# Softmax row sums by accumulating DMA transfers instead of GpSimd adds, and every low part of the probabilities on VectorE

## The chip, the core and the metric

One core of a Trainium2 chip runs one launch of the whole kernel. The metric is the device time of that launch in microseconds (us). Engines are named as in the profile: PE is TensorE (PEld its weight loads), DVE is VectorE, ACT is ScalarE, POOL is GpSimd, SP is SyncE.

## What is computed

One layer of a diffusion backbone for 512 latent tokens and 128 context tokens: modulation, a combined input projection, four heads of mLSTM, eight heads of attention, an output projection and an MLP. The change lies in the attention of the latent tokens alone: 512 queries against 512 latent and 128 context keys, all in 32-bit floats.

```python
def one(qi):
    s = jnp.einsum('bqhd,bkhd->bhqk', qi, kf) * scale
    p = jax.nn.softmax(s, axis=-1)
    return jnp.einsum('bhqk,bkhd->bqhd', p, vf)
```

## The kernel before

Weights and activations are cut into a high part (a cast to fp32r) and a low part (the value less its high part), and a product is made of two or three matmuls of these parts. `split` (L108) is the helper: the cast on ACT (L109), the subtraction on an engine that the caller names (L110).

The attention runs over 8 heads h and, in each, over 5 blocks j of 128 keys: a step (h, j). `weights(h, j)` (L978) multiplies the keys of the block by all 512 queries into a PSUM tile `st` (three matmuls, L982 to L984), takes the exponential on ACT into a tile `p` of 128 keys by 512 queries (L986), and splits it into `pu` (hi, lo). The subtraction of block 1 goes to POOL, those of the other four to DVE (L996). The row sum of the softmax needs the sum of the five tiles `p`: POOL adds them one after another into a tile `tot` of a pool of its own (L1001 to L1004, four adds a head). `values(h, j)` (L1007), two steps later, multiplies the values by hi and lo into `pv` (L1013), and with the last block `pvt` (L1017) copies half of it out. `sums(h)` (L1023), two steps after the last block, multiplies `tot` by a column of ones, which adds over the keys (L1027, tile `su`), and DVE takes the reciprocal (L1031). After every second head, `normalise` (L1034) scales the two heads' outputs.

Beside these the same steps prepare the next head: transposes `Tq` and `Tk` (L928, L937), their evacuation on ACT and DVE (L915, L916), a memset on POOL of one row of the key tile (L925), the row maxima `mx`, `nm` (L947, L948), and a context self-attention `cs`, `pc`, `co`. In the last three heads PE also has the first half of two output tiles `wo` (L637) to do, work that needs no attention result.

The tiles `p` and `pvt` come from one ring of 7 buffers (`tp`, tag "t", L89). The order of instructions on each engine is set by the program's scheduler, which uses an estimate of its own for how long things take; once set, every engine works its queue in order, and an instruction that waits holds up all behind it on that engine. A DMA issued on POOL stands in POOL's queue in the same way.

Of the kernel before, what the change touches and what calls it, by code (L numbers as in the profile page):

```python
# [14 lines left out]
ALU = mybir.AluOpType  # L15
# [7 lines left out]
TL = 512  # L23
# [31 lines left out]
def hybrid_layer(ctx: ExitStack, tc: tile.TileContext, d, o):  # L55
    nc = tc.nc
    V, S, G, PE = nc.vector, nc.scalar, nc.gpsimd, nc.tensor
# [20 lines left out]
    def U2(pool, name, dt=F32):  # L78
        return pool.tile([P, 8 * SW], dt, tag="u2", name=name)

    def view(t, off, *shape):
        n = int(np.prod(shape))
        v = t[:, off:off + n]
        if len(shape) == 1:
            return v
        names = "abcd"[:len(shape)]
        return v.rearrange("p (%s) -> p %s" % (" ".join(names), " ".join(names)), **dict(zip(names, shape)))

    def Tt(name, dt=F32, n=T):  # L89
        t = tp.tile([P, 646], dt, tag="t", name=name)  # L90
        return t[:, :n]

    def Pp(name, dt=F32, n=T):
        return tp.tile([P, 646], dt, tag="pp", name=name, bufs=2)[:, :n]
# [7 lines left out]
    def psS(name):  # L102
        return pss.tile([P, 512], F32, tag="s", name=name)

    def f(ap):
        return ap.bitcast(F32)

    def split(hi, lo, src, eng=V):  # L108
        S.copy(hi, src)  # L109
        return eng.tensor_tensor(out=lo, in0=src, in1=f(hi), op=ALU.subtract)  # L110
# [89 lines left out]
    def wget(key, ahead=3):  # L200
        i = state["get"]
        assert chunks[i][0] == key, (chunks[i][0], key)
        wsplit(i + 1)
        wdma(i + 4)
        wsplit(i + ahead)
        state["get"] += 1
        return ready.pop(i)
# [320 lines left out]
    for i in range(NT):  # L528
# [7 lines left out]
                      in_=st[:, KL + ROPE:KL + ROPE + 8].rearrange("p (a b) -> p a b", a=2))  # L536
        V.tensor_copy(out=gf[:, i, :].rearrange("p (a b) -> p a b", a=2)[:, :, 0:4],
                      in_=st[:, KL + ROPE + 8:KL + ROPE + 16].rearrange("p (a b) -> p a b", a=2))
# [48 lines left out]
    for ci, row in enumerate((r_a, r_e, r_w)):  # L587
        nt = NT if ci < 2 else 4
        pc = psS(f"pcol{ci}")
        for i in range(nt):  # L590
            PE.transpose(out=pc[:, i * 64:(i + 1) * 64], in_=row[:, i * P:(i + 1) * P], identity=ident[0:64, 0:64])
        V.tensor_copy(out=cols[:, ci, 0:nt].rearrange("p t d h -> p (t d) h"),
                      in_=pc[:, 0:nt * 64].rearrange("p (t b) -> p t b", b=32)[:, :, 0:4])
# [8 lines left out]
    for w in range(2):  # L602
# [4 lines left out]
                        in1=gs.unsqueeze(1).broadcast_to([P, NT, 2, 16]), op=ALU.mult)  # L607
# [195 lines left out]
    for k in range(2):  # L803
        pt = psD(f"ckt{k}")
        for i in range(NT):
# [17 lines left out]
                    in0=krn[:, 0:4].rearrange("p t (a b) -> p t a b", a=2)[:, :, ::-1, :],  # L823
                    in1=sg_[:, 1, 0:4].rearrange("p t (a b) -> p t a b", a=2), op=ALU.mult)
# [9 lines left out]
    for hf in range(2):  # L834
# [4 lines left out]
        hi, lo = wget(("kup", hf))  # L839
# [19 lines left out]
        for i in range(6):  # L859
            G.tensor_tensor(out=kn[:, i, :, 0:NOPE], in0=kn[:, i, :, 0:NOPE], in1=rsk[:, i, :].unsqueeze(2).broadcast_to([P, 4, NOPE]), op=ALU.mult)  # L860
            G.tensor_tensor(out=kn[:, i, :, NOPE:QK], in0=krr[:, i:i + 1, :].broadcast_to([P, 4, ROPE]),
                            in1=rsk[:, i, :].unsqueeze(2).broadcast_to([P, 4, ROPE]), op=ALU.mult)
# [12 lines left out]
    for hf in range(2):  # L875
# [4 lines left out]
        for i in range(NT):  # L880
            ps = (psS if i % 2 else psD)(f"qu{hf}{i}")
            for k in range(3):
                hi, lo = w0 if k < 2 else w1
# [8 lines left out]
            if i < 4:  # L892
                rt = view(Pp(f"rt{hf}{i}"), 0, 4, ROPE)
                V.tensor_tensor(out=rt.rearrange("p h (a b) -> p h a b", a=2),
                                in0=p4[:, :, NOPE:QK].rearrange("p h (a b) -> p h a b", a=2)[:, :, ::-1, :],
                                in1=sg_[:, 0, i:i + 1, :].rearrange("p t (a b) -> p t a b", a=2).broadcast_to([P, 4, 2, 16]), op=ALU.mult)
# [15 lines left out]
    prep, negm, cden, punit, tot, pacc = {}, {}, {}, {}, {}, {}  # L912
# [65 lines left out]
    def weights(h, j):  # L978
        qh, ql_, kh, kl_, qc, kc = prep[h]
        ps = psS(f"st{h}{j}")  # L980
        c = slice(j * P, (j + 1) * P)
        PE.matmul(ps, lhsT=kh[0:QK + 1, c], rhs=qh[0:QK + 1], start=True, stop=False)  # L982
        PE.matmul(ps, lhsT=kh[0:QK, c], rhs=ql_[0:QK], start=False, stop=False)
        PE.matmul(ps, lhsT=kl_[0:QK, c], rhs=qh[0:QK], start=False, stop=True)  # L984
        pj = Tt(f"p{h}{j}", n=TL)
        exp_ = S.activation(out=pj, in_=ps, func=AF.Exp)  # L986
        if h % 2:
            if j in (0, 2):
                u2s[j // 2] = view(U2(php, f"pu{h}{j}", F32R), 0, 5, TL)
            hi, lo = (u2s[j // 2][:, 2 * (j % 2) + k] for k in range(2)) if j < 4 else (u2s[k][:, 4] for k in range(2))  # L990
        else:
            pool, tag = ((whp, "wh"), (wlp, "wl"))[(5 * (h // 2) + j) % 2]
            u = pool.tile([P, 1024], F32R, tag=tag, name=f"pu{h}{j}")
            hi, lo = u[:, 0:TL], u[:, TL:2 * TL]
        punit[h, j] = hi, lo
        lo_ = split(hi, lo, pj, G if j == 1 else V)  # L996
        if j == 0:
            tot[h] = pj
        else:
            if j == 1:  # L1000
                first, tot[h] = tot[h], Pp(f"tot{h}", n=TL)  # L1001
            else:
                first = tot[h]
            G.tensor_tensor(out=tot[h], in0=first, in1=pj, op=ALU.add)  # L1004
        return exp_, lo_

    def values(h, j):  # L1007
# [53 lines left out]
    for n in range(len(steps) + DN):  # L1061
        if n < len(steps):
            h, j = steps[n]
            if h == 7 and j == 0:
                wsplit(state["get"] + 3)
            if (h, j) == (7, 4):
                w_first = wget(("out", 0))
                ps_first = psD("wo0")
                mmT(ps_first, w_first, kview(mhu * 2), kview(mlu * 2), KT, 0, 4)
            exp_, lo_ = weights(h, j)  # L1070
            if (h, j) in MSP:

# [27 lines left out]
        if 0 <= n - DN < len(steps):  # L1100
            h, j = steps[n - DN]
# [313 lines left out]
```

## Time and profile before

| | us |
|---|---|
| median of 3 runs (lowest, highest) | 888.99 (888.43, 892.16) |
| the profiled execution's own time | 886.29 |
| its span, first to last instruction | 884.2 |
| PE busy | 855.6 (97%) |
| DVE busy | 615.1 (70%) |
| ACT busy | 436.5 (49%) |
| POOL busy | 298.0 (34%) |

The profiled execution is 2.7 us below the median of the runs, and 2.1 us of its time lie outside its span. Busy shares are averages over stages with different limits; the steps of the change all lie in the attention, from about 300 to 396 us of the span.

### The profile page before, as it was taken

What the parts mean: (1) busy time and instruction counts of PE and PEld (TensorE: products, weight loads), DVE (VectorE), ACT (ScalarE), POOL (GpSimd) and SP (SyncE); (2) the same over time, 40 slices, a digit from 0 to 9 for tenths busy, and PEclk for the clock granted to TensorE, in tenths of its full rate; (3) what the DMA queues carried; (4) which work ended last, traced back from release to release, by engine and by line L of the source; (5) the groups of instructions that cost most, each with busy time, mean ns of one, the idle gap of its engine ahead of it and who ended that gap; (6) DMA issues with size and microseconds to landing.
All of it is one profiled execution on the core that took longest, in us unless ns stands there. A gap on an engine that the chain in (4) does not pass through costs nothing.

```text
span 884.2 us, 15211 instructions
## 1 busy us (share of the span) xinstructions
PE 855.6 (97%) x5805; PEld 800.7 (91%) x5805; DVE 615.1 (70%) x1226; ACT 436.5 (49%) x959; POOL 298.0 (34%) x311
## 2 busy tenths in 40 slices
PE   6999999999889999999989999999999999999998
PEld 5688799999777677889989999999999999999998
DVE  2654634546787889977898587595876949678673
ACT  3424326535764597955557153361544517254440
POOL 3100113313333575753743152241514215152300
PEclk9999999999999999999999999999999999999999
DMA  9842842231216200322141212122122221412132
GB/s 357 321 131 67 293 166 91 64 99 52 96 57 239 96 1 1 120 72 72 49 144 46 98 49 96 48 96 96 49 96 81 88 72 56 135 49 73 48 102 90
DMA packets 22328, 89.63 MB, mean 101 GB/s; under 512 B 3144, under 2 KB 3944, under 8 KB 18928
## 3 DMA queue, kind: packets, MB, share of 16 engines
q1 hardware_dynamic: 19440, 81.95, 26.8%
q0 software_dynamic: 1664, 4.26, 1.6%
q10 hardware_dynamic: 1152, 2.46, 0.7%
q8 instruction: 46, 0.75, 0.4%
q14 instruction: 26, 0.21, 0.1%
HBM read 85.33 MB, written 3.32 MB: 100 GB/s over the span
## 4 chain that ended last, share of the span: by engine, by line
PE 80%; DVE 8%; DMA 6%; ACT 3%; issue 2%; SPq 1%; POOL 0%; DVEq 0%; POOLq 0%; ACTq 0%
PE dn L637 25%; PE qk L637 6%; PE wo L637 5%; DMA st<-in_w_ada 3%; PE mo L637 2%; PE pv L1013 2%; DMA ad<-in_w_ada 2%; PE ada L389 2%; PE n L702 1%; PE up12M L1235 1%; PE up8M L1235 1%; PE up14M L1235 1%; PE up15M L1235 1%; PE up7M L1235 1%; PE up13M L1235 1%
## 5 line engine op out<-in xcount | busy, mean ns | idle before, releaser
L109 ACT CAST wh<-st 128x1024 fp32r<-128x1024 f32 (+4 forms) x69 | 69.3, 1007 | 103.0 <-PE dn L637 33.1
L1118 DVE SCALAR_TENSOR_TENSOR xr<-dn,modT,xr 128x320 f32<-128x320 f32 x64 | 35.3, 551 | 107.1 <-PE dn L637 107.1
L110 DVE TENSOR_TENSOR wl<-st,wh 128x1024 fp32r<-128x1024 f32 (+4 forms) x67 | 83.3, 1246 | 28.8 <-ACT wh L109 27.8
L637 PE MATMUL dn<-fh,wh 128*128 128x320 f32 x448 | 102.7, 310 | 0.3 <-ACT fh L1278 0.3
L637 PE MATMUL dn<-fh,wl 128*128 128x320 f32 x448 | 102.0, 309 | 0.0
L637 PE MATMUL dn<-fl,wh 128*128 128x320 f32 x448 | 98.6, 309 | 0.0
L109 ACT CAST wu<-S 128x512 fp32r<-128x512 f32 x64 | 38.1, 616 | 99.0 <-issue 92.3
L637 PEld LDWEIGHTS dn<-fh,wh 128*128 128x128 f32 x448 | 74.8, 188 | 2.2 <-PE dn L637 1.6
L637 PEld LDWEIGHTS dn<-fh,wl 128*128 128x128 f32 x448 | 74.9, 188 | 0.0
L637 PEld LDWEIGHTS dn<-fl,wh 128*128 128x128 f32 x448 | 74.0, 188 | 0.0
L1273 POOL TENSOR_TENSOR r<-r,rbs 128x320 f32<-128x320 f32 x32 | 37.5, 1183 | 106.6 <-DVE r L1251 106.6
L110 DVE TENSOR_TENSOR wu<-S,wu 128x512 fp32r<-128x512 f32 x64 | 57.5, 908 | 1.1 <-ACT wu L109 0.9
L1277 ACT ACTIVATE r<-r 128x192 f32<-128x192 f32 (+2 forms) x96 | 40.8, 466 | 25.8 <-DVE r L1251 17.1
L729 POOL TENSOR_TENSOR W<-ngb,mask 128x128 f32<-128x128 f32 x40 | 19.5, 502 | 67.0 <-DVE p L739 33.3
L1280 DVE TENSOR_TENSOR fl<-r,fh 128x320 fp32r<-128x320 f32 x56 | 38.2, 700 | 3.0 <-ACT r L1279 3.0
L1004 POOL TENSOR_TENSOR tot<-tot,p 128x512 f32<-128x512 f32 x24 | 37.2, 1549 | 5.9 <-ACT p L986 3.9
L109 ACT CAST wu<-pair 128x512 fp32r<-128x512 f32 x24 | 14.1, 615 | 43.8 <-PE dn L637 41.6
L110 DVE TENSOR_TENSOR pu<-p,pu 128x512 fp32r<-128x512 f32 x32 | 33.0, 1045 | 2.5 <-ACT pu L109 2.5
L219 POOL TENSOR_TENSOR S<-st,st 128x512 f32<-128x512 f32 x8 | 13.0, 1627 | 59.8 <-DVE wu L110 59.8
L1013 PE MATMUL pv<-pu,v 128*128 128x512 f32 x80 | 29.1, 427 | 2.1 <-DVE pu L110 2.0
L637 PE MATMUL wo<-mh,wh 128*128 128x320 f32 x128 | 29.6, 311 | 0.7 <-DVE xr L1120 0.7
L637 PE MATMUL qk<-hh,wl 128*128 128x320 f32 x128 | 29.9, 312 | 0.0
(487 smaller groups left out, 2436.8 us busy)
## 6 DMA issues: line engine op xcount, KB each, us to landing
st<-in_w_ada SPq DMA_DIRECT2D x16, 1024.0 KB, 5.6
st<-in_w_down SPq DMA_DIRECT2D x32, 512.0 KB, 3.4
ad<-in_w_ada SPq DMA_DIRECT2D x8, 1024.0 KB, 17.5
st<-in_w_up SPq DMA_DIRECT2D x16, 512.0 KB, 3.8
pair<-in_w_up SPq DMA_DIRECT2D x16, 512.0 KB, 4.8
st<-in_w_qko SPq DMA_DIRECT2D x12, 512.0 KB, 3.6
st<-in_w_out SPq DMA_DIRECT2D x8, 512.0 KB, 3.3
x<-in_x SPq DMA_DIRECT2D x4, 640.0 KB, 6.7
```

Of the source, the lines that this page charges most:

```text
L109: S.copy(hi, src)
L110: return eng.tensor_tensor(out=lo, in0=src, in1=f(hi), op=ALU.subtract)
L389: PE.matmul(ps[32 * j:32 * j + 32, 0:n], lhsT=sz[:, 2 * q + k, :], rhs=w[:, k, c], start=q == 0, stop=q == 3, tile_position=(0, 32 * j))
L637: PE.matmul(out[:, hf * 512:hf * 512 + HT], lhsT=wt[:, c], rhs=xt[k][:, hf * HT:(hf + 1) * HT], start=k0 == 0 and n == 0, stop=k1 == nk an ...
L729: G.tensor_tensor(out=W[:, dg:dg + P], in0=nb_[dr][:, j * P:(j + 1) * P], in1=mask[:, dr, :], op=ALU.add)
L1004: G.tensor_tensor(out=tot[h], in0=first, in1=pj, op=ALU.add)
L1013: PE.matmul(pacc[h], lhsT=v_u[hf][:, j, hh_, :], rhs=w, start=j == 0 and k == 0, stop=j == 4 and k == 1)
L1118: V.scalar_tensor_tensor(out=xr[m][:, 0:HT], in0=ps[:, 0:HT], scalar=modT[:, gi_ + m, 0:1], in1=xr[m][:, 0:HT], op0=ALU.mult, op1=ALU.add)
L1235: PE.matmul(ps, lhsT=w[:, c], rhs=b[k], start=k == 0 and w is hi and b is bh, stop=k == 3 and w is lo)
L1273: E.tensor_tensor(out=t, in0=t, in1=rbs[:, c], op=ALU.mult)
L1277: S.activation(out=t[:, c0:c1], in_=t[:, c0:c1], func=AF.Relu, bias=r[n][:, w:w + 1])
L1280: V.tensor_tensor(out=FL[n][:, c], in0=t, in1=f(FH[n][:, c]), op=ALU.subtract)
```

## The change

The adds on POOL are gone. The tile `p` of block 0 becomes the accumulator itself, and each of the other four blocks is added to it by a DMA, issued on POOL, that reads `p` of the block and adds it onto the destination. The low part of block 1 is made on DVE, as the others are. The separate tile `tot` falls away.

```diff
@@ -993,15 +993,12 @@
             u = pool.tile([P, 1024], F32R, tag=tag, name=f"pu{h}{j}")
             hi, lo = u[:, 0:TL], u[:, TL:2 * TL]
         punit[h, j] = hi, lo
-        lo_ = split(hi, lo, pj, G if j == 1 else V)
+        lo_ = split(hi, lo, pj)
         if j == 0:
             tot[h] = pj
         else:
-            if j == 1:
-                first, tot[h] = tot[h], Pp(f"tot{h}", n=TL)
-            else:
-                first = tot[h]
-            G.tensor_tensor(out=tot[h], in0=first, in1=pj, op=ALU.add)
+
+            G.dma_start(out=tot[h], in_=pj, accum_op=ALU.add)
         return exp_, lo_
```

From L1004 on, lines of the changed kernel have numbers lower by 3 (the add of L1004 is the DMA of L1001, `su` of L1027 is L1024).

POOL's queue from head 0 to the start of head 1, before. Names carry head and block (`p01` is head 0, block 1); in brackets stand the engines or DMA transfers (DMASW) waited for.

```order
L1004 TENSOR_TENSOR tot0_3291<-p00_3265,p01_3286 128x512 [waits DMASW6_49,Activation_49]
L110 TENSOR_TENSOR pu01_3288<-p01_3286,pu01_3288 128x512 [waits Activation_49]
L1004 TENSOR_TENSOR tot0_3291<-tot0_3291,p02_3314 128x512 [waits Activation_49,Pool_49]
L925 MEMSET qk2_3384 1x640 [waits PE_49,Pool_49]
L1004 TENSOR_TENSOR tot0_3291<-tot0_3291,p03_3336 128x512 [waits Activation_49,Pool_49]
L1004 TENSOR_TENSOR tot0_3291<-tot0_3291,p04_3361 128x512 [waits Activation_49,Pool_49]
L1004 TENSOR_TENSOR tot1_3406<-p10_3379,p11_3402 128x512 [waits DMASW7_49,Activation_49]
```

The same place in the changed kernel.

```order
L1001 DMA p00_3265<-p01_3286 128x512 [waits DMASW2_49,DVE_49]
L925 MEMSET qk2_3383 1x640 [waits PE_49,Pool_49]
L1001 DMA p00_3265<-p02_3313 128x512 [waits DMASW3_49,DMASW2_49,Activation_49]
L1001 DMA p00_3265<-p03_3335 128x512 [waits DMASW3_49,Activation_49]
L1001 DMA p00_3265<-p04_3360 128x512 [waits DMASW4_49,Activation_49]
L1001 DMA p10_3378<-p11_3401 128x512 [waits DMASW6_49,DVE_49]
L1001 DMA p10_3378<-p12_3440 128x512 [waits DMASW7_49,DMASW6_49,Activation_49]
```

The adds are DMAs now; the second, third and fourth of a head each wait for the transfer of the one before them, while the first waits for DVE (the low part of block 0, which reads the accumulator before it is changed) and not for the last transfer of the head before.

PE's queue around the row sum of head 0, before.

```order
L982 MATMUL st11_3398<-qk1_3270 128x512
...
L961 MATMUL cs1_3418<-qkc1_3271 128x128 [waits PE_49]
L947 MATMUL mx20_3449<-qk2_3384 128x320 [waits Activation_49]
...
L1027 MATMUL su0_3430<-ones_99,tot0_3291 128x2 [waits Activation_49,Pool_49]
...
L982 MATMUL st12_3438<-qk1_3270 128x512 [waits Activation_49]
...
L947 MATMUL mx21_3453<-qk2_3384 128x320 [waits DVE_49]
```

The same place in the changed kernel.

```order
L982 MATMUL st11_3397<-qk1_3270 128x512
...
L961 MATMUL cs1_3416<-qkc1_3271 128x128 [waits PE_49]
L947 MATMUL mx20_3447<-qk2_3383 128x320 [waits Activation_49]
...
L947 MATMUL mx23_3471<-qk2_3383 128x320 [waits DVE_49]
...
L1024 MATMUL su0_3428<-ones_99,p00_3265 128x2 [waits DMASW5_49]
...
L982 MATMUL st12_3436<-qk1_3270 128x512
...
L1010 MATMUL pv1_3455<-pu10_3380,v0_2616 128x512 [waits Activation_49]
```

The row sum of head h still stands between blocks 1 and 2 of head h + 1, with three more row maxima ahead of it, and waits for the transfer of block 4 in place of POOL; the scores of blocks 2, 3 and 4 of the next head stand behind it. The place is the same in every head but the last.

## Rows read from the trace of the kernel before

**Rows 1.** The page: busy tenths, granted clock and DMA share in 40 slices.

```profile
PE   6999999999889999999989999999999999999998
...
PEclk9999999999999999999999999999999999999999
DMA  9842842231216200322141212122122221412132
```

**Rows 2.** Busy time of each engine between the row sums of heads 0, 1, 4, 7.

```profile
core 0: us, PE busy (x) PEld busy (x) DVE busy (x) ACT busy (x) POOL busy (x), PEclk, DMA share, GB/s
312.35:322.85 10.50, 10.50 (x65) 8.61 (x63) 8.75 (x15) 9.52 (x22) 8.14 (x6) 1.00 0.00 1
322.85:359.00 36.15, 33.82 (x206) 26.52 (x204) 34.13 (x46) 30.14 (x64) 24.35 (x19) 1.00 0.00 1
359.00:394.35 35.35, 35.35 (x230) 29.40 (x229) 32.52 (x44) 27.96 (x57) 23.97 (x17) 1.00 0.34 120
```

**Rows 3.** The chain that ended last, in order of time: row sums.

```profile
312.35 0.79 PE su L1027 x8
...
322.85 0.79 PE su L1027 x8
...
359.00 0.79 PE su L1027 x8
...
394.35 0.79 PE su L1027 x8
```

**Rows 4.** Groups of instructions between 300 and 396 us (count, busy us, mean ns, idle before).

```profile
L1004 POOL TENSOR_TENSOR tot<-tot,p 128x512 f32<-128x512 f32 x24 | 37.2, 1549 | 5.9 <-ACT p L986 3.9 <-ACT mix L976 1.0
L110 DVE TENSOR_TENSOR pu<-p,pu 128x512 fp32r<-128x512 f32 x32 | 33.0, 1045 | 2.5 <-ACT pu L109 2.5
...
L1004 POOL TENSOR_TENSOR tot<-p,p 128x512 f32<-128x512 f32 x8 | 12.2, 1519 | 16.5 <-ACT p L986 13.5 <-DVE mix L1048 3.0
L110 POOL TENSOR_TENSOR pu<-p,pu 128x512 fp32r<-128x512 f32 x8 | 11.1, 1384 | 5.8 <-ACT pu L109 5.8
```

**Rows 5.** Instructions on tile p: shortest, median and longest, ns.

```profile
L986 ACT ACTIVATE p<-st x40: 582/597/617, 301.4 to 392.0; 128x512 f32<-128x512 f32 x40
...
L110 DVE TENSOR_TENSOR pu<-p,pu x32: 671/1038/1784, 303.9 to 393.3; 128x512 fp32r<-128x512 f32 x32
```

**Rows 6.** Timeline of head 0's first low part, and around head 1's row sum.

```profile
303.94 0.68 DVE L110 TENSOR_TENSOR pu<-p,pu 128x512 fp32r<-128x512 f32 x1
...
322.69 0.95 PE L1027 MATMUL su<-ones,tot 128*128 128x2 f32 x8
...
323.78 1.20 DVE L110 TENSOR_TENSOR pu<-p,pu 128x512 fp32r<-128x512 f32 x1
323.88 0.40 PE L982 MATMUL st<-qk 97*128 97x512 f32 x1
...
324.35 0.39 PE L984 MATMUL st<-qk 96*128 96x512 f32 x1
```

**Rows 7.** DMAs issued on POOL: KB each, median us from issue to landing.

```profile
ngb<-ngd POOLq DMA_DIRECT2D x8, 320.0 KB, 3.8
...
cst<-in_C POOLq DMA_DIRECT2D x4, 128.0 KB, 2.6
out_C<-co POOLq DMA_DIRECT2D x4, 128.0 KB, 2.2
...
late<-in_late POOLq DMA_DIRECT2D x1, 256.0 KB, 4.1
```

**Rows 8.** L671, eight 320 KB loads on POOL: issue time (ns), and us to landing.

```profile
L671 POOL DMA_DIRECT2D ngb<-ngd x8: 551/568/608, 104.2 to 222.5; - x8
...
DMA to landing us min/median/max: 3.5/3.8/7.5
```

**Rows 9.** L584, and POOL's timeline there: a DMA waiting for another's landing.

```profile
DMA to landing us min/median/max: 4.5/4.5/4.5
...
99.33 0.51 POOL L584 DMA_DIRECT2D ngd<-ru  x1
99.82 0.50 POOL L585 DMA_DIRECT2D ngd<-ru  x1
104.15 1.11 POOL L671 DMA_DIRECT2D ngb<-ngd  x2 [3.83 <-DMA ngd<-ru]
```

## The prediction

> **What bounds the kernel now.** I read the 40 slices first: PE is busy for nine tenths or more in most of them, its granted clock is full in all, and the DMA engines stand nearly still in slices 15 and 16, which lie in the first half of the attention [rows 1]. All that the change touches lies there, so I went on to the attention alone. The chain of waits shows the row sums of heads 0 and 7 at 312.35 and 394.35 us [rows 3]: 82.0 us for seven heads, 11.7 us a head. Busy time by stretch says what fills them: of the 82.0 us PE works 79.7, and is idle for 2.3 only, all of it in the middle stretch, where DVE works 34.1 of 36.2 us [rows 2]. So the stage is PE's, with DVE close behind, and POOL (56.5 of 82.0 us) has slack. This fixes the most that relief of any other engine can bring here: about 2.3 us.
>
> **What is taken away.** POOL loses 32 adds (37.2 + 12.2 us) and 8 subtractions (11.1 us) [rows 4]. POOL is not the limit, so this is worth nothing by itself. It may help DVE: its subtraction takes 0.67 us at best and 1.05 us in the mean [rows 4, 5]. If POOL's work causes all of that spread, 32 subtractions win 32 x 0.37 = 12 us of DVE time; if none of it, nothing. The 8 subtractions that DVE takes over cost 8 x 0.67 = 5.4 to 8 x 1.05 = 8.4 us. DVE's balance thus lies between -6.6 and +8.4 us, over a stage in which PE, on the sum below, waits far longer for something else. I count it at nothing; without that cover, up to 8 us of it would show, since DVE is idle for only 2 us of the middle stretch.
>
> **What is added: a chain of transfers.** Before, four adds of 1.5 us stood one behind another [rows 4]. Now each is a transfer whose successor waits, at the head of POOL's queue, until it has landed; the first transfer of the next head is not held. At the far end PE's row sum waits for the fourth, and behind that row sum in PE's queue stand the scores of blocks 2, 3 and 4 of the next head, without which the next head's second transfer has nothing to add. Head after head closes a loop: landing, row sum, scores, exponential, three transfers, landing.
>
> Call L the time from the issue of one transfer to its landing. A link is L plus the time until the waiting DMA starts. The trace has one such pair: issued at 99.33 us, landed 4.5 us later, at 103.83, and the waiting DMA starts at 104.15 [rows 9]. A link is L + 0.3.
>
> *First head.* Its first transfer waits for the low part of block 0, done at 303.94 + 0.68 = 304.6 us [rows 6]. Four transfers with three gaps: the fourth lands at 305.5 + 4L.
>
> *Each further head.* From landing to the next head's second transfer: the row sum 0.95 us, the scores 0.86 (323.88 to 324.74) [rows 6], the exponential 0.60 [rows 5], and some 0.4 for the handovers (0.24 lies between row sum and scores [rows 6]): 2.8 us. The first transfer of that head was issued behind the fourth of the last and has landed by then. Three transfers and two gaps follow: 3L + 0.6. A head takes 3L + 3.4.
>
> *Sum.* The row sum of head 7 comes at 305.5 + 4L + 7 x (3L + 3.4) = 329.3 + 25L, against 394.35: a shift of 25L - 65. What follows that row sum is the same work as before, so the shift goes through to the end. PE's own 11.7 us a head fit into the loop's wait as soon as 3L + 3.4 exceeds 11.7, that is from **L = 2.8 us** on.
>
> *How large is L?* No accumulating transfer is in this trace. The plain ones of POOL's queue bound it: 2.2 to 2.6 us for 128 KB, 3.5 to 3.8 for 320 KB, 4.1 for the one of 256 KB, 7.5 for the slowest [rows 7, 8]. From 2.4 at 128 KB to 3.65 at 320 KB is 1.25 us for 192 KB; a plain 256 KB would take 3.2. Here the destination has to be read as well, another 256 KB, 1.7 us at that slope. I take **L = 4.9**, an estimate from these rows, since a plain transfer of the same size already took 4.1. Ends: 2.2, if the second read is free and SBUF at both ends is quick, and 7.5 or more, if the additions run slower than the copies.
>
> With L = 4.9 the shift is 57.5 us: 886.3 + 57.5 = 943.8 for the profiled execution, which stands 2.7 us below the median shown. **I predict 946 us.** A head would take 18.1 us.
>
> The Trainium skill, DMA: Bandwidth & Descriptors, section "Anatomy of one DMA — SWDGE (gpsimd) path", gives 2.0 us plus bytes over 436 GB/s, an estimate of 2.6 us for 256 KB. By it the loop would be shorter than PE's work and the change free, the first rival below. The trace does not agree with it: for 320 KB it would be 2.75, measured were 3.5 at best [rows 8].
>
> *What else moves.* The issue of a transfer holds POOL for about 0.57 us (8 loads of 128 rows, 551 to 608 ns [rows 8]); it runs inside L. The memset for the head after next stands between two transfers and waits out one link; ACT's evacuation of the transposes waits for it, but that is needed only by the next head's scores, most of a loop later. The ring of 7 buffers now holds each tile until its transfer has landed, and the accumulator until the row sum; blocks 2 to 4 of the next head come after that row sum, so they find the older transfers landed. If they did not, one more link a head, about 5 us, would join the loop. In heads 5 to 7 PE's first half of the output tiles now stands before the row sum of head 6 and fills a wait; it brings nothing, as the loop, not PE, sets the end.
>
> **The rivals.** *No change: the transfers are quick* (L of 2.2 to 2.6, from the 128 KB rows [rows 7]). Then PE keeps 11.7 us a head, and only the first chain shows: at 2.6 it lands at 315.9 instead of 312.35, at 2.2 at 314.3. The time is 891 to 893. It decides below L = 2.8. For it: the DMA engines are idle in the first half of the stage [rows 1]. Against it: twice the size of those rows, and a second read. Beyond it lies a gain, of at most PE's 2.3 idle us [rows 2], if DVE's relief is real and the first chain is covered.
>
> *The second read is hidden*: L = 3.2, a plain 256 KB. Shift 15, time 904, still slower.
>
> *The additions are slow*: L above 7.5. At 7.5 the shift is 122 and the time 1011; each further microsecond costs 25. For it: one 320 KB load took 7.5 [rows 8]. Against it: that one left together with a second [rows 9], and in the first half of this stage other traffic is 1 GB/s [rows 2]. DVE might also hold up POOL's making of descriptors: it is busy for 34.1 of 36.2 us [rows 2], yet the issues in the trace spread by 57 ns only [rows 8].
>
> The Trainium skill, SBUF — State Buffer, section "SBUF: two separate sides", says that a DMA issued from GpSimd can sit without descriptors while VectorE runs an operation that holds the port the two share. No run here shows such a case yet; it would make L longer, and so speaks against the change.
>
> **How the numbers follow.** The forecast, L between 2.8 and 7.5, gets 0.80; of this 0.15 is the hidden second read. Additions slower than that get 0.10, quick transfers 0.10: 0.07 for no change and 0.03 for a gain. The range runs from 898 (L of about 3, from 25 x 3 - 65 = 10) to 1015 (7.6) and leaves out the two end cases. A measurement of this kernel tells about 0.5%, 4.4 us, from no change. Faster 0.03, same 0.07, slower 0.90.
>
> **What the profile after would show.** Right: POOL's adds and its `pu` rows gone; `su` rows about 18 us apart; PE idle before `su`, released by a DMA, for some 6 us a head; 32 transfers on POOL of 256 KB with a median landing near 4.9 us; POOL's second, third and fourth DMA of a head waiting for a DMA; the stretch after the last `su` as long as before. DVE's `pu` subtractions nearer 0.67 us would show the relief. Wrong would be: `su` 11.7 us apart and PE still full (quick transfers); or PE waiting for ACT or DVE before the scores, with the transfers long landed (the ring or DVE took over); or a head of 3L + 3.4 that does not fit the landing time measured, which would break the loop itself.

## The result and the profile after

The changed kernel takes **937.1 us** (median of four runs, 931.4 to 938.2), the kernel before 888.7 (887.8 to 892.2): a ratio of 1.0546 [1.0514, 1.0578]. The profiled execution took 937.72 us, with a span of 935.9 against 884.2 before, 51.7 us more.

The page of the changed kernel: the span, TensorE's 40 slices and its granted clock, then two of its groups and one kind of transfer.

```profile
span 935.9 us, 15214 instructions
...
PE   6999999999899779777998999999999999999998
...
PEclk9999999999999798778998999999999999999999
...
L110 DVE TENSOR_TENSOR pu<-p,pu 128x512 fp32r<-128x512 f32 x40 | 27.0, 682 | 14.4 <-ACT pu L109 14.2
L1024 PE MATMUL su<-ones,p 128*128 128x2 f32 x64 | 12.3, 315 | 25.0 <-DMA p<-p 24.7
...
p<-p POOLq DMA_DIRECT2D x32, 256.0 KB, 3.3
```

Four things stand against the rows of before. PE waited 24.7 us for transfers before the row sums. Its slices show holes at 7 where they were full, and there the *granted clock* has fallen too [rows 1]. VectorE's 40 subtractions take 27.0 us, less than the 33.0 of 32 before [rows 4]. And a transfer lands in 3.3 us, not in the 4.9 of the sum.

The stretches of the changed kernel from each row sum to the next (heads 0 to 7), then three stretches behind the last one.

```profile
core 0: us, PE busy (x) PEld busy (x) DVE busy (x) ACT busy (x) POOL busy (x), PEclk, DMA share, GB/s
319.25:334.55 15.30, 14.06 (x58) 11.03 (x58) 4.69 (x8) 8.28 (x17) 3.20 (x4) 0.73 0.36 64
334.55:351.10 16.55, 11.09 (x64) 8.81 (x64) 12.39 (x22) 10.94 (x24) 4.62 (x6) 0.90 0.40 69
351.10:366.35 15.25, 15.14 (x77) 11.84 (x78) 5.81 (x10) 7.80 (x15) 3.20 (x4) 0.77 0.36 63
366.35:383.91 17.56, 11.91 (x66) 8.95 (x66) 14.53 (x24) 13.49 (x30) 4.62 (x6) 0.95 0.38 66
383.91:407.61 23.70, 17.13 (x80) 12.40 (x80) 11.66 (x19) 10.59 (x22) 3.77 (x5) 0.72 0.60 161
407.61:427.47 19.86, 19.86 (x115) 17.21 (x116) 11.10 (x16) 11.18 (x20) 3.43 (x4) 0.87 0.49 109
427.47:440.94 13.47, 6.98 (x32) 4.54 (x30) 2.95 (x5) 4.45 (x9) 2.99 (x8) 0.84 0.45 98
440.94:456.00 15.06, 14.32 (x87) 13.39 (x88) 4.83 (x11) 3.87 (x5) 0.00 (x0) 0.80 0.00 1
...
504.00:508.00 4.00, 3.40 (x15) 2.58 (x13) 4.00 (x8) 1.89 (x5) 1.59 (x2) 0.62 0.02 6
508.00:512.00 4.00, 3.96 (x17) 3.96 (x17) 1.98 (x5) 1.01 (x2) 0.00 (x0) 0.53 0.00 0
```

The seven stretches make 121.7 us where before had 82.0 [rows 3]. With the first row sum 6.9 us late, the last one is 46.6 us late (440.94 against 394.35). From there to the end it takes 495.0 us against 489.9, 5.1 more, and 46.6 + 5.1 = 51.7 is the whole difference. Of the 5.1 us, 2.8 are lost by the first matmul of the MLP (496.8 against 447.4); the row 440.94:456.00 shows TensorE busy there at a clock of 0.80. The rest is lost behind it, where from 504 to 512 us the clock is low once more (0.62 and 0.53), after TensorE had been idle for 1.8 us for ScalarE and not for a transfer.

POOL's timeline of the changed kernel (start, duration, the idle time before with its releaser): the loop from head 0 to head 1, the first transfer of head 2, a disturbed transfer of head 5, and the second transfers of heads 6 and 7.

```profile
315.89 1.75 POOL L1001 DMA_DIRECT2D p<-p  x2 [2.96 <-DMA p<-p]
323.53 0.86 POOL L1001 DMA_DIRECT2D p<-p  x1 [5.88 <-ACT p L986]
327.33 0.86 POOL L1001 DMA_DIRECT2D p<-p  x1 [2.94 <-DMA p<-p]
331.14 0.86 POOL L1001 DMA_DIRECT2D p<-p  x1 [1.89 <-ACT pu L109]
336.33 0.86 POOL L1001 DMA_DIRECT2D p<-p  x1 [4.33 <-DVE rd L1028]
...
397.98 0.86 POOL L1001 DMA_DIRECT2D p<-p  x1 [2.63 <-ACT qk L955]
411.89 0.86 POOL L1001 DMA_DIRECT2D p<-p  x1 [8.60 <-ACT p L986]
...
430.15 0.86 POOL L1001 DMA_DIRECT2D p<-p  x1 [6.07 <-ACT p L986]
```

This is the loop that was forecast. The pair at 315.89 is head 0's fourth transfer and head 1's first. The fourth lands at 319.2, the row sum runs at 319.25, the scores and the exponential follow, and head 1's second transfer leaves at 323.53, then one every 3.8 us. Head 1's row sum is at 334.55. A link is 3.3 + 0.5 us, not L + 0.3. The transfer at 397.98 landed after 9.6 us, beside two loads of 1,280 KB that SP issued at 396.58.

### The profile page after: what moved, and what is told of

It is laid out like the page before. It is cut to its first block, busy times and chain, and to the rows that moved or that the text cites. A ratio compares the mean times of both kernels' runs of the same rounds, so it can differ in the third digit from the quotient of the medians.

```text
span 935.9 us, 15214 instructions
## 1 busy us (share of the span) xinstructions
PE 879.7 (94%) x5805; PEld 817.1 (87%) x5805; DVE 607.8 (65%) x1234; ACT 437.8 (47%) x959; POOL 265.1 (28%) x303
## 4 chain that ended last, share of the span: by engine, by line
PE 50%; DVE 2%; issue 1%; DMA 0%; ACT 0%; DVEq 0%; POOLq 0%
PE dn L637 24%; PE wo L637 4%; PE up1M L1232 1%; PE up12M L1232 1%; PE up4M L1232 1%; PE up8M L1232 1%; PE up14M L1232 1%; PE up15M L1232 1%; PE up7M L1232 1%; PE up13M L1232 1%; PE up11M L1232 1%; PE up9M L1232 1%; PE up5M L1232 1%; PE up3M L1232 1%; PE up10M L1232 1%; PE up2M L1232 1%
## 5 line engine op out<-in xcount | busy, mean ns | idle before, releaser
L1001 POOL DMA_DIRECT2D p<-p x32 | 27.6, 893 | 105.8 <-ACT p L986 46.6
L986 ACT ACTIVATE p<-st 128x512 f32<-128x512 f32 x40 | 23.8, 598 | 47.6 <-PE st L984 46.6
L110 DVE TENSOR_TENSOR pu<-p,pu 128x512 fp32r<-128x512 f32 x40 | 27.0, 682 | 14.4 <-ACT pu L109 14.2
L1024 PE MATMUL su<-ones,p 128*128 128x2 f32 x64 | 12.3, 315 | 25.0 <-DMA p<-p 24.7
L1024 PEld LDWEIGHTS su<-ones,p 128*128 128x128 f32 x64 | 11.9, 276 | 26.9 <-DMA p<-p 26.2
L1010 PE MATMUL pv<-pu,v 128*128 128x512 f32 x80 | 32.2, 467 | 1.5 <-ACT pu L109 1.1
## 6 DMA issues: line engine op xcount, KB each, us to landing
ad<-in_w_ada SPq DMA_DIRECT2D x8, 1024.0 KB, 17.5
```

Of the source, the lines that this page charges most:

```text
L1001: G.dma_start(out=tot[h], in_=pj, accum_op=ALU.add)
L1010: PE.matmul(pacc[h], lhsT=v_u[hf][:, j, hh_, :], rhs=w, start=j == 0 and k == 0, stop=j == 4 and k == 1)
L1024: PE.matmul(ps[:, 2 * i:2 * i + 2], lhsT=t[:, i * P:(i + 1) * P], rhs=ones[:, 0:2], start=True, stop=True)
```

## Experiments

**e1_low_only** does one half of the change alone: VectorE makes all low parts, the additions stay on POOL.

```diff
-        lo_ = split(hi, lo, pj, G if j == 1 else V)
+        lo_ = split(hi, lo, pj)
```

> The kernel before, with only the low part of block 1 moved from GpSimd to VectorE; the adds stay on GpSimd. Theory (the chain of transfers is the whole loss): no measurable change, 886 to 892 us against 889, and VectorE's 40 subtractions take 0.8 to 1.05 us each. Rival (the eight more subtractions on VectorE, which was busy 34.1 of 36.2 us in the middle stretch, cost their time): 894 to 897 us.

Measured: 893.9 us against 887.5, 1.0067 [1.0044, 1.0091], 6.4 us more: nearly what the rival said. The waits of e1_low_only from 300 to 420 us (total, times, longest).

```profile
PEld pv L1013 <- DVE pu L110: 9.0, 15, 1.4
...
PE pv L1013 <- DVE pu L110: 4.0, 9, 0.9
```

VectorE's eight further subtractions are not hidden where POOL still adds: the mean of all 40 is 1,039 ns there, against 682 in the changed kernel. In e2_dma_only below, where POOL keeps its subtractions and has no additions, it is 688 ns. So it is POOL's *additions* that stretch VectorE's subtractions, not POOL's subtractions.

**e2_dma_only** does the other half: transfers as in the change, block 1's low part back on POOL.

```diff
-        lo_ = split(hi, lo, pj)
+        lo_ = split(hi, lo, pj, G if j == 1 else V)
```

> The changed kernel with the low part of block 1 back on GpSimd; the sums stay with the accumulating transfers. Theory: the whole loss is here, 932 to 945 us, a little above the changed kernel if GpSimd's 1.3 us subtraction lands between two links. Rival (the low part shares in the loss): 925 us or less.

Measured: 940.7 us, 1.0593 [1.0557, 1.0629], about as long as the whole change (the intervals overlap). The loss lies in the transfers.

**e4_plain_copy** takes the addition out of the transfers: they overwrite their destination.

```diff
-            G.dma_start(out=tot[h], in_=pj, accum_op=ALU.add)
+            G.dma_start(out=tot[h], in_=pj)
...
```

The row sums are therefore left out, and VectorE clamps what it finds at 1.0, one small instruction more a head (not shown in the cut; e10_half has it too).

> The changed kernel with plain copies in place of the accumulating transfers: each overwrites the accumulator, so the row sums are left out (VectorE clamps what it finds, off the path); same sizes, queue and waits. Theory (reading the destination is priced as I forecast, with a good part of the transfer): the copies land in 2.4 us or less against 3.3, and the time falls by 20 us or more. Rival (the addition itself costs next to nothing, fixed parts make up the 3.3): 3.0 to 3.3 us to landing, an issue near 0.57 us instead of 0.86, and 928 to 938 us.

Measured, in one run: 907.9 us against 888.1. The transfers of e4_plain_copy (ns of an issue, then us to landing):

```profile
L1001 POOL DMA_DIRECT2D p<-p x32: 536/538/632, 303.2 to 411.7; - x32
...
DMA to landing us min/median/max: 2.2/2.3/7.4
```

The addition costs 3.3 - 2.3 = 1.0 us of each landing, of which 0.32 in the issue (857 ns against 538 at the median). But a loss of 20 us is left at 2.3 us, where the prediction's sum had none.

**e10_half** sends only half the columns (128 KB).

```diff
-            G.dma_start(out=tot[h], in_=pj, accum_op=ALU.add)
+            G.dma_start(out=tot[h][:, 0:TL // 2], in_=pj[:, 0:TL // 2], accum_op=ALU.add)
...
```

> The changed kernel with each accumulating transfer cut to half of the columns (128 KB); the second half of the row sums is that of block 0 alone, VectorE clamps the sums at 1.0. The plain copies of 256 KB landed in 2.3 us, the accumulating ones in 3.3. Theory (the addition costs by the byte, and the price is the loop's): landing falls by half of that 1.0 us, to 2.7 to 2.9 us; each of some 25 links is 0.4 to 0.6 shorter, 10 to 15 us, and the clock gives some back: 918 to 928 us. Rival (the addition is a fixed cost of each transfer, as is most of the landing): 3.1 to 3.3 us and 932 to 939 us.

Measured: 916.9 us, 1.0334 [1.0304, 1.0364], and this landing in the trace of e10_half:

```profile
DMA to landing us min/median/max: 2.6/2.7/6.5
```

Half the bytes save 0.6 us of 3.3, so the larger part of a landing is not paid by the byte. The landing is what the theory said, the time a little lower. That the addition costs by the byte is not shown: its 0.32 us in the issue stay (857 ns at the median here too), and a plain copy of 128 KB, which would split the 0.6 us into copy and addition, was not run. The three runs are a sweep over L: 2.3 gives +19.8 us, 2.7 gives +29.0, 3.3 gives +48.4 (by the medians). That is 23 and 32 us per microsecond of landing. The prediction's 25 lies between them; its zero, at L = 2.6, was wrong.

**e7_fill** asks what the clock does. Before each set of row sums PE runs 14 matmuls of 512 columns into the same bank, which the row sums overwrite; they need no transfer and run while PE would wait.

```diff
+        for i in range(14):
+            PE.matmul(ps, lhsT=identr, rhs=v_u[0 if h < 3 else 1][:, 0].rearrange("p a b -> p (a b)"), start=True, stop=True)
         for i in range(4):
             PE.matmul(ps[:, 2 * i:2 * i + 2], ...
```

> The changed kernel with 14 idle-filling matmuls of 512 columns ahead of each row sum on TensorE, into the PSUM bank that the row sum then overwrites (3.3 us of work a head that computes nothing). Theory (part of the loss is TensorE's clock, 0.50 for several microseconds after each long wait): the granted clock stays at 1.0 or nearly, the row sums and scores take 0.95 and 0.86 us again, and the time falls by 5 to 12 us in spite of the added work. Rival (the clock only slows work that has slack): 937 us or more.

Measured: 920.6 us, 1.0364 [1.0327, 1.0401]: **16.5 us less** than the changed kernel (the theory said 5 to 12), with 27.7 us more work on its bottleneck engine. But the filling is not all that differs. With it the scheduler chose another order; TensorE's timeline of e7_fill around the first row sum:

```profile
313.47 3.42 PE L1024 MATMUL su<-v,kc 128*128 128x512 f32 x14
316.73 0.39 PE L982 MATMUL st<-qk 97*128 97x512 f32 x1
...
318.47 0.40 PE L982 MATMUL st<-qk 97*128 97x512 f32 x1
...
321.18 1.05 PE L1026 MATMUL su<-ones,p 128*128 128x2 f32 x8 [1.38 <-DMA p<-p]
```

The scores of blocks 2 and 3 of head 1 stand ahead of head 0's row sum here, and not behind it. The same holds for one block at head 2's row sum and for two at head 5's; at the others the scores stay behind. So e7_fill also opens the loop in three of seven heads, and its gain is not the clock's alone. The stretches of e7_fill between its row sums (four of the seven; columns as above):

```profile
321.18:334.72 13.54, 12.48 (x62) 9.71 (x62) 6.88 (x12) 7.33 (x16) 3.77 (x5) 0.87 0.46 79
...
350.71:364.28 13.57, 13.57 (x92) 11.38 (x90) 8.77 (x14) 10.02 (x21) 3.74 (x5) 1.00 0.39 69
364.28:378.54 14.26, 14.09 (x78) 11.35 (x77) 11.27 (x18) 11.73 (x24) 4.06 (x5) 1.00 0.43 75
...
418.07:432.42 14.35, 14.35 (x78) 11.60 (x77) 3.24 (x6) 4.67 (x9) 2.80 (x5) 1.00 0.32 56
```

Where the clock is full, a head takes 13.6 to 14.4 us. The prediction's 3L + 3.4 gives 13.3 for the L of 3.3 that was measured; of these stretches the last two keep the forecast order of row sum and scores. The last row sum is at 432.42, 8.5 us earlier than in the changed kernel, and from there to the end it takes 489.6 us, about as before the change; but 20 more of the output projection's matmuls, some 3 us, stand ahead of that row sum here, 68 in place of 48.

How the clock falls without the filling, in the changed kernel around the first row sum (columns as above):

```profile
312.00:313.00 1.00, 0.35 (x2) 0.30 (x2) 1.00 (x2) 0.95 (x3) 0.85 (x1) 1.00 0.00 0
313.00:314.00 1.00, 0.81 (x4) 0.30 (x2) 1.00 (x3) 1.00 (x4) 0.00 (x0) 0.89 0.57 100
...
316.00:319.00 3.00, 0.00 (x0) 0.00 (x0) 0.64 (x1) 0.00 (x0) 1.64 (x2) 0.50 0.58 99
...
323.00:327.00 4.00, 4.00 (x15) 3.12 (x14) 1.39 (x2) 2.07 (x4) 0.86 (x1) 0.50 0.36 66
327.00:328.00 1.00, 1.00 (x8) 0.95 (x7) 0.00 (x0) 0.27 (x1) 0.67 (x1) 0.79 0.00 0
```

The clock is down to 0.50 (1.2 of 2.4 GHz) when PE stands still for the transfer, and stays there while PE is busy without a pause from 320 to 327 us. The wait is thus paid a second time: the row sum takes 1.87 us where it took 0.95, and what stands behind it runs slower too, inside the loop. The changed kernel itself has the price. From the row sum to the second transfer of the next head it takes 4.28 us in heads 1, 3, 5 and 6, at 0.50 (319.25 to 323.53), and 2.68 in head 7 (427.47 to 430.15), where the clock was full:

```profile
319.25:323.53 4.28, 4.28 (x14) 3.80 (x15) 0.18 (x1) 0.86 (x2) 0.00 (x1) 0.50 0.24 42
427.47:430.15 2.68, 2.68 (x18) 2.36 (x17) 0.18 (x1) 0.86 (x2) 0.00 (x0) 1.00 0.58 197
```

That is 4 x 1.6 = 6.4 us inside the loop, for the same row sum, scores and exponential.

**e6_xr_late** asks what the loads beside the transfers cost. The two loads of 1,280 KB are held back until the last normalisation.

```diff
     for k in range(2):
+        V.tensor_copy(out=view(xu2[k], 0, 4, T)[:, 0, 0:1], in_=mix_a[:, 3, 0:1])
         nc.sync.dma_start(out=view(xu2[k], 0, 4, T), ...
```

> The changed kernel with the two 1280 KB loads of the residual held back until the last head is normalised (a one-column copy into each buffer makes them wait). Theory (they lengthened two links, to 9.6 and 6.2 us, and the chain is the path): all links of heads 5 and 6 that lay beside them are near 3.3 us again and the time falls by 6 to 10 us, to 927 to 931, less what the later loads cost the output projection. Rival (those links were hidden): 935 us or more.

Measured: 934.8 us, 1.0522 [1.0489, 1.0555], hardly less than the changed kernel and nearly what the rival said. The chain that ended last in e6_xr_late, transfers of heads 5, 6 and 7 and, later, the load:

```profile
396.25 3.25 DMA p<-p
...
409.37 6.17 DMA p<-p
...
416.61 6.11 DMA p<-p
...
443.51 5.58 DMA xr<-in_x
```

Without the loads head 5's landings are back at 3.3 us (396.25, where 9.6 stood). Two later ones still take 6.1 to 6.2, beside the loads of the output projection's weights, which I did not move. The last row sum comes 6.8 us earlier (434.11), and 5.7 us of it are given back behind it, where the chain now waits for the late load. So the lengthened landings are real, but moving these loads buys nothing.

**e5_two_acc** shortens the chain: blocks 1 and 2 are added to block 0, block 4 to block 3, 24 transfers, and PE's row sums add the two accumulators.

```diff
-        if j == 0:
-            tot[h] = pj
+        if j in (0, 3):
+            tot[h, j > 2] = pj
...
+            for k in range(2):
+                PE.matmul(ps[:, 2 * i:2 * i + 2], lhsT=t[k][:, i * P:(i + 1) * P], rhs=ones[:, 0:2], start=k == 0, stop=k == 1)
```

> The changed kernel with two accumulators a head: blocks 1 and 2 are added to block 0, block 4 to block 3, and the row sum adds both on TensorE; 24 transfers, the longest chain two. Theory (the loop is as long as its chain): the fourth link and the third fall away, landing and block 4's exponential are 4 to 5 us apart, and the row sum hardly waits: 892 to 900 us, of which 4 to 7 are TensorE's four more small matmuls a head. Rival (what costs is any transfer ahead of the row sum, not the length of the chain): 915 us or more.

Measured: 904.9 us, 1.0193 [1.0155, 1.0232], between theory and rival. PE waited 1.8 us before the row sums in place of 24.7. This run shortens the loop and POOL's queue (three transfers a head, not four) at once, so it does not tell the two apart; the next one does.

**e3_late_sum** opens the loop in another way: the row sums stand three steps later in PE's order, and the accumulators have a pool of their own.

```diff
-        pj = Tt(f"p{h}{j}", n=TL)
+        pj = (Tt if j else Pp)(f"p{h}{j}", n=TL)
...
-    DV, DS, DN = 2, 2, 9
+    DV, DS, DN = 2, 5, 9
```

> The changed kernel with TensorE's row sum three steps later, behind the scores of block 4 of the next head, and the accumulator of each head in the pool that held the sums before. Theory (the loss is the loop landing, row sum, scores, next transfer): the loop is cut, and what stays is GpSimd's queue, three links of 3.8 us and one issue of 0.9, 12.3 us a head against TensorE's 11.7: 892 to 905 us. Rival (the transfers bound the stage by themselves, four links of 3.8 us a head): 15.2 us a head, about 917 us.

Measured: 920.1 us, 1.0364 [1.0329, 1.0398], far above the theory and close to the rival. POOL's timeline of e3_late_sum, head 0 to 1 and beside the loads:

```profile
315.28 1.75 POOL L1001 DMA_DIRECT2D p<-p  x2 [2.89 <-ACT p L986]
320.65 0.86 POOL L1001 DMA_DIRECT2D p<-p  x1 [3.58 <-DMA p<-p]
...
328.29 1.74 POOL L1001 DMA_DIRECT2D p<-p  x2 [2.98 <-DVE mix L1016]
...
374.35 0.86 POOL L1001 DMA_DIRECT2D p<-p  x1 [3.56 <-PE Tk L937]
385.30 0.86 POOL L1001 DMA_DIRECT2D p<-p  x1 [9.78 <-DMA p<-p]
```

Here the transfers follow one another from 304 to 420 us almost without a pause. From one pair (a head's fourth transfer and the next head's first) to the next it is 13.0 us (315.28 to 328.29), more than PE's 11.7 a head, and the link of 11 us beside the loads (374.35 to 385.30) has nothing to hide behind. With the loop open, the chain itself is the bound: PE still waited 22.3 us for transfers before its row sums.

**e8_late_two** joins the two (two accumulators, row sums three steps later).

> Two accumulators a head and the row sum three steps later, together. Theory (no wait for a transfer is left on TensorE, nor a drop of its clock): 892 to 899 us, the rest over 889 being the four more small matmuls a head, about 0.8 us each head. Rival (GpSimd's queue of transfers still bounds a head): 905 us or more, as with two accumulators alone.

Measured: 899.0 us, 1.0131 [1.0099, 1.0163]. Its profile, of the shortest of the four executions, has a clock of 1.000, and no engine's wait there was ended by a transfer of the sums. Its row sums:

```profile
L1025 PE MATMUL su<-ones,p 128*128 128x2 f32 x128 | 15.0, 244 | 0.0
```

They cost 15.0 us where 64 cost 7.6 before. The 7.4 us more stand against 9.4 by which its span (893.6) is longer; that they are the cause of it is not shown.

**e11_late_add** takes these 7.4 us away: as e8_late_two, but VectorE adds the two accumulators.

```diff
+        V.tensor_tensor(out=t[0], in0=t[0], in1=t[1], op=ALU.add)
```

> Two accumulators a head (24 transfers) and the row sums three steps later, as in e8_late_two, but VectorE adds the two accumulators (8 additions of some 0.65 us) before one set of row sums, so TensorE has its 64 small matmuls again in place of 128. Theory (with the loop gone what was left of the loss, 11.6 us, was mostly the doubled row sums): 886 to 893 us, within 0.5% of before. Rival (what was left comes from the transfers beside the loads, or the addition waits in VectorE's queue for the landing and holds the low parts behind it): 896 to 905 us.

Measured: 900.1 us, 1.0142 [1.0116, 1.0168]: the rival. Waits of e11_late_add from 300 to 445 us:

```profile
DVE p L1023 <- DMA p<-p: 11.8, 6, 5.1
...
PE pv L1010 <- DVE pu L110: 5.4, 1, 5.4
```

The wait for the landing has moved into VectorE's queue, and the low part behind it held PE once for 5.4 us. So what e8_late_two still loses stays open. No version with transfers beat the kernel before.

## Why the prediction was right, and where not

*Direction, place and mechanism: right.* PE is the bound, POOL's work is worth nothing, and the transfers close a loop over PE's in-order queue: PE waits for the fourth transfer before the row sum, and the next head's second transfer for an exponential whose scores stand behind that row sum. e2_dma_only puts the whole loss on the transfers. But the loop is only part of it. Opened alone (e3_late_sum), it gives back 17 of the 48 us; the chain of transfers alone then takes 13.0 us a head, more than PE's 11.7, which the prediction did not consider. With two accumulators, so a shorter chain, e5_two_acc and e8_late_two give back 32 and 38. 946 was forecast, 937.1 measured; a head was to take 18.1 us and took 17.4 in the mean.

*L = 4.9: wrong.* It is 3.3. The step that failed is "1.7 us at that slope" for reading the destination: the addition cost 1.0 us (e4_plain_copy). And the base of 3.2 for a plain 256 KB was too high: 2.3. Both came from loads and stores of other sizes [rows 7, 8]; none of them was a copy within SBUF. The rival "quick transfers" thus had the right plain landing, and the rival "second read is hidden" the right L for the wrong reason.

*With L = 3.3 the formula gives a shift of 17.5 us, and 46.6 came, plus 5.1 behind it.* So two errors cancelled: the nearness of 946 to 937.1 is luck. One of the prediction's own signs of being wrong came with it, a head that does not fit 3L + 3.4 at the landing time measured. The excess lies in the heads, 121.7 us against 7 x 13.3 = 93.1; the first head's 305.5 + 4L = 318.7 came at 319.2. What the working left out:

- *The clock.* It was not priced at all. From landing to the next head's second transfer it took 4.3 us (319.2 to 323.53) in heads 1, 3, 5 and 6 where 2.8 was reckoned, 6.1 us in all. "What follows that row sum is the same work as before, so the shift goes through to the end" fails in the same way: at 0.80 of the clock it is not the same time. What more the clock costs is not separated, as e7_fill changed the order too.
- *The first transfer of an even head.* It "has landed by then", the prediction says. In heads 2 and 4 it left only after the previous landing (336.33, after one at 334.4, and 368.47, after one at 366.2), and the fourth link joined the loop: 6.5 us. VectorE's queue has a part in it: in head 4 the low part of block 0, which the first transfer waits for, stands behind the reciprocal of the previous row sum (lines below). In e7_fill it stands ahead of it (362.13, the reciprocal at 365.94), and the transfer leaves at 363.12, before the previous landing. In head 2 the low part stands ahead of the reciprocal and was late all the same, behind 15.3 us of PE at a clock of 0.73; that this made it late is not shown.
- *A third transfer.* In head 5 it waited until 394.16 for the exponential of block 3, whose scores stood behind the matmuls of a normalisation: 2.2 us.
- *Lengthened landings.* Heads 5 and 6 took 23.7 and 19.9 us. Landings of 9.6 and 7.5 us in the loop, in place of 3.3, are 10.5 of the 17.0 us by which they exceed 2 x 13.3. The prediction looked at the quiet first half of the stage [rows 2] only.
- *The gap of 0.3* in a link was 0.5, two links a head, 7 x 2 x 0.2 = 2.8 us.

These parts, with the 10.5 us of the long landings, make 6.1 + 6.5 + 2.2 + 10.5 + 2.8 = 28.1 of the 121.7 - 93.1 = 28.6 us. VectorE's timeline of the changed kernel at the first low part of head 4:

```profile
367.41 0.18 DVE L1028 RECIPROCAL rd<-su 128x4 f32<-128x4 f32 x1 [0.32 <-PE su L1024]
367.51 0.66 DVE L110 TENSOR_TENSOR pu<-p,pu 128x512 fp32r<-128x512 f32 x1
```

Nor did PE wait some 6 us in every head: it waited 3.8 to 6.1 us before the row sums of heads 0, 2, 4, 5 and 7 and at most 0.2 before the other three.

*The point of no loss, L = 2.8: wrong.* At 2.3 the kernel is still 19.8 us slower. In that run PE's waits for transfers are short (5.5 us in all), but its clock falls to 0.8 in some heads, and undisturbed heads take 12.9 to 13.5 us against PE's 11.7. It is not the clock alone: the stretches of 12.9 and 13.4 (327.64 to 340.52, 353.83 to 367.22) have a full one. There, as in the changed kernel, the first transfer leaves only after the row sum (329.75 and 356.07), and four links follow one another where the formula has three. How much of these 20 us is clock and how much the order of the scores was not separated.

*VectorE's balance: its good end.* 33.0 to 27.0 us is a gain of 6.0, near the -6.6 of the text, and the subtraction is at 0.68, as it said. e1_low_only showed the other end: with POOL's additions kept, 6.4 us are lost. That the balance counts nothing held because PE waited for something else.

*VectorE holding up the descriptors* hardly showed: while VectorE was at work beside them, single landings with no load beside them lay at 3.2 to 3.3 us, but for one at 3.4 and two at 3.5 to 3.7 (issued at 368.47 and 372.54), whose cause is open.

The Trainium skill, DMA: Bandwidth & Descriptors, "Anatomy of one DMA — SWDGE (gpsimd) path", gives 2.0 us plus bytes over 436 GB/s, an estimate of 2.6 us for 256 KB, with no word on additions in that section. The plain copy took 2.3, less than the estimate; the accumulating one took 3.3, and the measurement decides.

## What to carry to other kernels

Here a chain of dependent transfers cost its whole latency and 0.5 us per link. Find who stands behind its end in an in-order queue, and whether what stands there feeds the next chain: if so, the latency closes a loop, and "the DMA engines are idle" is no cover. When a change makes TensorE wait for a few microseconds again and again, price its clock too: here the work after the wait ran at 0.50. Before a filling is credited with the clock's price, see whether the order of the instructions stayed the same. And check a forecast by its parts, as a total can be near for two wrong reasons.

## What the runs showed of the hardware

- An accumulating transfer of 256 KB within SBUF lands in 3.3 us and one of 128 KB in 2.7; a plain one of 256 KB in 2.3. POOL spends 0.86 us on issuing it, at either size, 0.54 on the plain one, and the next dependent one starts 0.5 us after the landing.
- Landings rise to 9.6 us beside two loads of 1,280 KB, and to 7.5 beside loads of 512 KB.
- The granted clock stood at 0.50 in a wait of 3 us and through the 7 us of work without a pause behind it (320 to 327). From a row sum to the transfer that follows from it, the same work took 4.28 us at 0.50 and 2.68 at the full clock.
- VectorE's subtraction of 128x512 takes 0.68 to 0.69 us in the mean without POOL's additions and 1.04 to 1.05 beside them.
